# Four operand offsets in a decoder-layer kernel changed to two, and two of four weight combinations moved from VectorE to GpSimd

## The chip, the cores and the metric

The kernel runs on one core of a Trainium2 chip. The metric is the device time of one execution in microseconds (us): the median of three runs. One more execution was taken with the profiler on; all rows shown here come from it. Engines are named as in the profile: PE is TensorE's matmul, PEld its weight load, DVE is VectorE, ACT is ScalarE, POOL is GpSimd, SP is SyncE.

## The reference, cut to what matters

One decoder layer on 512 positions of width 2048, all in float32. Attention heads and a state-space mixer stand side by side, then a SwiGLU block of inner width 5632, then a last norm.

```
proj = rmsnorm(h) @ w_in                     # q, k, v, u: 4 x 1024
attn_out = dilated attention(q, k, v)        # 8 heads of 128
ssm_out  = y * sigmoid(y @ w_glu + b_glu)    # y: state-space scan over u, then GELU
h = h + concat(attn_out, ssm_out) @ w_out
hn = rmsnorm(h)
h = h + (silu(hn @ w_gate) * (hn @ w_up)) @ w_down
return rmsnorm(h)
```

## The kernel before

**Three matmuls for one product.** Everything is kept transposed: 128 features on the partitions, 512 positions along the row. A float32 operand is split into a high part (ScalarE copies it to the type that TensorE takes, `whi` for weights) and a rest (VectorE subtracts the high part from the raw value, `wlo`). A product is then three matmuls, lines 109 to 111 in `mm3`: high by high, high by rest, rest by high. `wsplit` makes the two parts of a 128x512 block of weights in buffers that are used in turn, five of each kind (`HB = 5`); the raw weights come by DMA from SP into four buffers of 1024 columns (`RAW = 4`).

**Slots for the moving operand.** The activations that stream through TensorE lie in slots of 1088 float32 a partition, of which 1024 are used: the high part and the rest. `laid(pool_, tag, name, bufs, o)` (line 167) gives a slot whose data begin `o` elements into it. There are three pools of such slots. In `ring` (tags A0, A1) lie the normed input `x`, then `attn`, `ssm`, `c1`, `c3`; in `ring2` (tag B) `ysp`, then `c2`; in `mp` (tags a, C) the SwiGLU outputs `m` and `c4`. Slots have one size, so two tiles of one pool and one `o` lie alike. The offsets are:

| operand | products | columns a matmul | pool | offset before |
|---|---|---|---|---|
| `x` | u, q, k, v | 512 | ring | 0 |
| `ysp` | glu | 512 | ring2 | 4 |
| `attn` | oa (first half of w_out) | 512 | ring | 8 |
| `ssm` | os (second half of w_out) | 256 | ring | 40 |
| `c1`, `c3` | gu products 1, 2, 5, 6 | 256 | ring | 48 |
| `c2` | gu products 3, 7 | 256 | ring2 | 48 |
| `c4` | gu product 4 | 256 | mp | 52 |
| `m` | dn (w_down), all groups but the last | 512 | mp | 0 |
| `m` | dl (w_down, last group) | 256 | mp | 48 |

**Gate and up with seven products.** For each of 44 tiles of 128 inner features, `gu(f)` computes gate and up together as a 2 by 2 block product in Winograd's form: seven products with combined weights and combined activations in place of eight. Each tile has two halves (`hh`), each with two DMAs of raw weights, `r1` (a11, a21) and `r2` (a22, a12). In a half, the weights of the products are, in the order in which they run on PE:

- A = a11 (product 1), C = a22 (product 4), B = a12 (product 2), as they come;
- D = a21 + a22 (product 5), written over a22;
- E = a11 - a21 (product 7), written over a21;
- F = D - a11 (product 6), written over a11;
- G = a12 - F (product 3), written over a12.

Each product is 12 matmuls of 256 columns: four blocks of weights, three matmuls each. The order of the lines in the program is that of `gu` (lines 738 to 749); the order of the instructions on each engine is set by the framework's scheduler, and each of DVE, ACT and POOL executes its own list in order. Lines 753 to 764 combine the seven results from four PSUM banks (seven adds of 256 columns and a multiply on VectorE) and split the output `m`.

**Order of the phases.** Eleven groups of four tiles. After the first tile of a group comes `down` for the group before: 16 output tiles of 12 matmuls with 512 columns. So on PE 192 matmuls of 512 columns alternate with runs of four tiles, 8 halves of 84 matmuls with 256 columns. Of the first five tiles the products A and B run ahead of the others (`gu_first`), while the loop at line 770 forms `c2`, `c3`, `c4` with VectorE and with GpSimd, which does four subtractions a step. The last `down` (`dl`) runs in two halves of 256 columns.

Of the kernel before, what the change touches and what calls it, by code (L numbers as in the profile page):

```python
# [15 lines left out]
ALU = mybir.AluOpType  # L16
# [19 lines left out]
def _emit(tc, a, y):  # L36
    nc = tc.nc
    act, dve, pool, pe = nc.scalar, nc.vector, nc.gpsimd, nc.tensor
    open_pools = {}

    def opened(name, **kw):
        cm = tc.tile_pool(name=name, **kw)
        open_pools[name] = cm
        return cm.__enter__()
# [4 lines left out]
    def tt(out, in0, in1, op, eng=None):  # L49
        (eng or dve).tensor_tensor(out=out, in0=in0, in1=in1, op=op)  # L50
# [23 lines left out]
    def acc(name):  # L74
        return psum.tile([128, 512], F32, tag="acc", name=name, bufs=5)
# [3 lines left out]
    def bank(name):  # L79

        turn[0] += 1
        return aux([128, 512], name) if turn[0] % 8 in (2, 5, 7) else acc(name)
# [6 lines left out]
    def split(hi, lo, raw):  # L89
        act.activation(hi, raw, AF.Copy)  # L90
        tt(lo, raw, hi.bitcast(F32), ALU.subtract)

    def wraw(src, name):
        raw = wpool.tile([128, 1024], F32, tag="raw", name="raw_" + name, bufs=RAW)
        nc.sync.dma_start(raw, src)
        return raw
# [16 lines left out]
    def ftile(ps, chunks, acts, name):  # L113
        n = len(chunks)
        for c, src in enumerate(chunks):
            ws = wchunk(src, f"{name}_{c}")
            for k in range(8):
                hi, lo = ws[k // 4]
                sl = slice(128 * (k % 4), 128 * (k % 4) + 128)
                mm3(ps, hi[:, sl], lo[:, sl], acts[8 * c + k], c == 0 and k == 0, c == n - 1 and k == 7)  # L120
# [43 lines left out]
    ring = opened("ring", bufs=1)  # L164
    SLOT = 1088

    def laid(pool_, tag, name, bufs, o):

        t = pool_.tile([128, SLOT], F32R, tag=tag, name=name, bufs=bufs)
        return t[:, o:o + 1024].rearrange("p (a b) -> p a b", a=2)  # L170

    def slot(tag, name, shift=0):
        return laid(ring, tag, name, 8, shift)
# [123 lines left out]
    for n in (1, 2, 4):  # L297
# [4 lines left out]
        t_ = pt[:, :, :n]  # L302
# [233 lines left out]
    ring2 = opened("ring2", bufs=1, side="right")  # L536
# [20 lines left out]
    ysp = []  # L557
    for b in range(8):
        yt = wpool.tile([128, 512], F32, tag="sq", name=f"yt{b}", bufs=4)
        nc.sync.dma_start(yt, sy[b].rearrange("p i c -> p (i c)"))  # L560
        t_ = laid(ring2, "B", f"ysp{b}", 8, 4)
        split(t_[:, 0, :], t_[:, 1, :], yt)
        ysp.append(t_)


    attn = []
    def scores(h):
        Pb = [slot("A1", f"P{h}_{i}").bitcast(F32) for i in range(2)]
        Tb = [slot("A1", f"PT{h}_{i}").bitcast(F32) for i in range(2)]
        for i in range(4):  # L570
            n = 128 * (i + 1)
            P = Pb[i // 2][:, i % 2, :]
            sps = aux([128, 512], f"sc{h}_{i}")
            pe.matmul(sps[:, :n], qs[h][:, 128 * i:128 * i + 128], ks[h][:, 0:n], start=True, stop=True)
            st = cpool.tile([128, 4], F32, tag="st", name=f"st{h}_{i}", bufs=4)
            dve.tensor_tensor_reduce(out=P[:, :n], in0=sps[:, :n], in1=mask[:, 512 - n:512], scale=1.0, scalar=-3e38,
                                     op0=ALU.add, op1=ALU.max, accum_out=st[:, 0:1])
            ts(st[:, 1:2], st[:, 0:1], -SCALE)
            act.activation(P[:, :n], P[:, :n], AF.Exp, bias=st[:, 1:2], scale=SCALE, accum_out=st[:, 2:3])
            dve.reciprocal(st[:, 3:4], st[:, 2:3])  # L580
            ts(P[:, :n], P[:, :n], st[:, 3:4])
        return Pb, Tb

    nxt = scores(0)
    for h in range(NH):
        Pb, Tb = nxt
        if h + 1 < NH:
            nxt = scores(h + 1)
        po = acc(f"po{h}")
        for step in "t0 t1 t2 p0 t3 p1 p2 p3".split():  # L590
            j = int(step[1])
            w = 512 - 128 * j
            PT = Tb[j // 2][:, j % 2, :]
            if step[0] == "t":
                tp = acc(f"tp{h}_{j}")
                for i in range(j, 4):
                    pe.transpose(tp[:, 128 * (i - j):128 * (i - j) + 128], Pb[i // 2][:, i % 2, 128 * j:128 * j + 128], ident)
                act.activation(PT[:, :w], tp[:, :w], AF.Copy)
            else:
                pe.matmul(po[:, 128 * j:512], vs[j][:, 128 * h:128 * h + 128], PT[:, :w], start=j == 0, stop=j == 3)  # L600
        o = slot("A0", f"attn{h}", 8)
        act.activation(o[:, 0, :], po, AF.Copy)
        tt(o[:, 1, :], po, o[:, 0, :].bitcast(F32), ALU.subtract)
        attn.append(o)


    ssm = []
    for f in range(8):
        ps = acc(f"glu{f}")
        ftile(ps, [a["w_glu"][f]], ysp, f"glu{f}")  # L610
        g_ = wpool.tile([128, 512], F32, tag="sq", name=f"gate{f}", bufs=4)
        act.activation(g_, ps, AF.Sigmoid, bias=bg[:, f:f + 1])
        yt = wpool.tile([128, 512], F32, tag="sq", name=f"yr{f}", bufs=4)
        nc.sync.dma_start(yt, sy[f].rearrange("p i c -> p (i c)"))
        z = wpool.tile([128, NC_, T], F32, tag="sq", name=f"gz{f}", bufs=4)
        tt(z.rearrange("p c i -> p i c"), yt.rearrange("p (i c) -> p i c", i=T), g_.rearrange("p (i c) -> p i c", i=T), ALU.mult)
        o = slot("A1", f"ssm{f}", 40)
        split(o[:, 0, :], o[:, 1, :], z.rearrange("p c i -> p (c i)"))
        ssm.append(o)
    closed("v")  # L620
# [6 lines left out]
    h = [hall[:, f, :] for f in range(KT)]  # L627
# [10 lines left out]

    def comb(tag, name, pool_=None, bufs=8):

        return laid(pool_ or ring, tag, name, bufs, 52 if tag == "C" else 48).rearrange("p a (h t) -> p a h t", h=2)

    early = {}

# [63 lines left out]
    def product(banks, i, hh, wh, wl):  # L708
        b_, j = REG[i]
        ps = banks[b_][:, E[j]]  # L710
        for k in range(4):
            sl = slice(128 * k, 128 * k + 128)
            mm3(ps, wh[:, sl], wl[:, sl], operand(i, 4 * hh + k), hh == 0 and k == 0 and i in (1, 5, 7, 4),
                hh == 1 and k == 3 and i in (2, 3, 6, 4))
# [16 lines left out]
    def gu(f, bank0=None):  # L731
        banks = [bank0 or bank(f"gu{f}_0")] + [bank(f"gu{f}_{i}") for i in range(1, 4)]
        for hh in range(2):
            r1 = wraw(a["w_gu"][f, hh, 0], f"r1_{f}_{hh}")
            r2 = wraw(a["w_gu"][f, hh, 1], f"r2_{f}_{hh}")
            a11, a21, a22, a12 = r1[:, W0], r1[:, W1], r2[:, W0], r2[:, W1]
            if bank0 is None:
                product(banks, 1, hh, *wsplit(a11, f"A{f}_{hh}"))
            product(banks, 4, hh, *wsplit(a22, f"C{f}_{hh}"))
            if bank0 is None:  # L740
                product(banks, 2, hh, *wsplit(a12, f"B{f}_{hh}"))
            tt(a22, a21, a22, ALU.add)
            product(banks, 5, hh, *wsplit(a22, f"D{f}_{hh}"))
            tt(a21, a11, a21, ALU.subtract)
            product(banks, 7, hh, *wsplit(a21, f"E{f}_{hh}"))
            tt(a11, a22, a11, ALU.subtract)
            product(banks, 6, hh, *wsplit(a11, f"F{f}_{hh}"))
            tt(a12, a12, a11, ALU.subtract)
            product(banks, 3, hh, *wsplit(a12, f"G{f}_{hh}"))
        P = {i: banks[b_][:, E[j]] for i, (b_, j) in REG.items()}  # L750
        g_ = wpool.tile([128, 512], F32, tag="sq", name=f"gt{f}", bufs=4)
        u_ = wpool.tile([128, 512], F32, tag="sq", name=f"up{f}", bufs=4)
        act.activation(g_[:, E[0]], P[1], AF.Copy)
        tt(u_[:, E[0]], g_[:, E[0]], P[6], ALU.add)
        tt(g_[:, E[0]], g_[:, E[0]], P[2], ALU.add)
        tt(g_[:, E[1]], u_[:, E[0]], P[5], ALU.add)
        tt(g_[:, E[1]], g_[:, E[1]], P[3], ALU.add)
        act.activation(g_, g_, AF.Silu)
        tt(u_[:, E[0]], u_[:, E[0]], P[7], ALU.add)
        tt(u_[:, E[1]], u_[:, E[0]], P[5], ALU.add)  # L760
        tt(u_[:, E[0]], u_[:, E[0]], P[4], ALU.add)
        tt(g_, g_, u_, ALU.mult)
        o = laid(mp, "a", f"m{f}", 4, 48 * (f >= 4 * (NPH - 1)))
        split(o[:, 0, :], o[:, 1, :], g_)
        return o
# [37 lines left out]
    for p in range(NPH):  # L803
        ms = []
        for q in range(4):
            f = 4 * p + q
# [114 lines left out]
```

## Time and profile before

| | |
|---|---|
| median of 3 runs | 2116.21 us (2115.62 to 2118.56) |
| the profiled execution's own time | 2112.28 us |
| its span, first to last instruction | 2110.5 us |
| mean granted TensorE clock | 0.986 |
| instructions | 35164, of which 13522 matmuls |

A row of the page's first part gives busy time, share of the span and number of instructions. A row of a timeline gives start, duration, engine, line, operation and tiles (out<-in). Matmuls overlap: one of 256 columns is shown 0.28 us long, while the next starts some 0.11 us behind its start, so the pace of PE is read from the distances of the starts, or from the number of matmuls in a stretch, and not from durations. The count in a stretch takes in those that reach over its ends: 1.7 (512 columns) or 2.4 (256 columns) too many, by duration over distance.

### The profile page before, as it was taken

How to read it: one execution, taken by the hardware profiler on the slowest of the kernel's cores; microseconds unless marked ns; L12 is line 12 of the kernel's file. 1: busy time of each engine (PE TensorE's matmuls, PEld its weight loads, DVE VectorE, ACT ScalarE, POOL GpSimd, SP SyncE). 2: the span in 40 equal slices, each digit the busy share in tenths (PEclk: the TensorE clock that was granted, in tenths of full speed). 3: DMA queues.
4: the chain of work that ended last, by engine and by line, in shares of the span. 5: the costliest groups of instructions: out<-in, count | busy, mean ns of one | idle time of the engine just before them, and what ended most of it. 6: DMA issues, size and time to landing. Idle time of an engine off the chain costs nothing.

```text
span 2110.5 us, 35164 instructions
## 1 busy us (share of the span) xinstructions
PE 2053.3 (97%) x13522; PEld 1858.4 (88%) x13522; DVE 1535.6 (73%) x2932; ACT 865.6 (41%) x1523; POOL 198.1 (9%) x172
## 2 busy tenths in 40 slices
PE   7899999999999979999999999999999999999996
PEld 5688888877889979899998989899998989999896
DVE  8835897555436989687786968687686868778686
ACT  5222222346325645344443535344352535444354
POOL 4533102300002360000000000000000000000002
PEclk9999999999999989999999999999999999999998
DMA  6443234623324614323232223323232332323232
GB/s 222 127 121 112 92 102 140 178 81 125 125 91 169 206 65 140 121 100 120 82 129 90 101 101 120 111 90 130 85 124 83 111 110 101 120 88 124 90 121 80
DMA packets 117193, 244.24 MB, mean 116 GB/s; under 512 B 39040, under 2 KB 57312, under 8 KB 117024
## 3 DMA queue, kind: packets, MB, share of 16 engines
q1 hardware_dynamic: 107808, 239.88, 33.8%
q10 hardware_dynamic: 9216, 2.10, 0.5%
q8 instruction: 106, 1.74, 0.3%
q14 instruction: 63, 0.52, 0.1%
HBM read 229.77 MB, written 9.03 MB: 113 GB/s over the span
## 4 chain that ended last, share of the span: by engine, by line
PE 87%; DVE 7%; issue 2%; DMA 1%; ACT 1%; SPq 0%; POOL 0%; DVEq 0%; ACTq 0%; POOLq 0%
PE gu L109 12%; PE gu L111 12%; PE gu L110 12%; PE dn L110 7%; PE dn L109 7%; PE dn L111 7%; PE lps L437 1%; PE q L111 1%; PE q L110 1%; PE oa L111 1%; PE oa L109 1%; PE oa L110 1%; PE q L109 1%; PE v L550 1%; PE v L552 1%
## 5 line engine op out<-in xcount | busy, mean ns | idle before, releaser
L110 PE MATMUL dn<-m,whi_dn 128*128 128x512 f32 x640 | 249.0, 389 | 0.0
L109 PE MATMUL dn<-m,whi_dn 128*128 128x512 f32 x640 | 248.8, 389 | 0.0
L111 PE MATMUL dn<-m,wlo_dn 128*128 128x512 f32 x640 | 248.8, 389 | 0.0
L50 DVE TENSOR_TENSOR h<-h,dn 128x512 f32<-128x512 f32 x160 | 109.9, 687 | 172.5 <-PE dn L111 171.3
L90 ACT ACTIVATE whi_dn<-raw_dn 128x512 fp32r<-128x512 f32 x160 | 100.9, 632 | 240.5 <-PE dn L110 208.2
L50 DVE TENSOR_TENSOR raw_r<-raw_r,raw_r 128x512 f32<-128x512 f32 x264 | 182.5, 691 | 2.2
L111 PEld LDWEIGHTS dn<-m,wlo_dn 128*128 128x128 f32 x640 | 120.2, 188 | 24.9
L109 PEld LDWEIGHTS dn<-m,whi_dn 128*128 128x128 f32 x640 | 120.2, 188 | 24.6
L110 PEld LDWEIGHTS dn<-m,whi_dn 128*128 128x128 f32 x640 | 120.2, 188 | 24.5
L50 POOL TENSOR_TENSOR h<-h,ssf 128x256 f32<-128x256 f32 x12 | 10.7, 920 | 1300.1 <-ACT ssf L160 1300.1
L50 DVE TENSOR_TENSOR wlo_dn<-raw_dn,whi_dn 128x512 fp32r<-128x512 f32 x160 | 109.8, 687 | 17.6 <-ACT whi_dn L90 16.5
L109 PE MATMUL gu<-c,whi_C 128*128 128x256 f32 x352 | 99.8, 284 | 1.9 <-ACT c L90 1.6
L111 PE MATMUL gu<-c,wlo_E 128*128 128x256 f32 x352 | 98.8, 281 | 2.8 <-DVE wlo_E L50 2.8
L109 PE MATMUL gu<-c,whi_D 128*128 128x256 f32 x352 | 98.3, 279 | 2.7 <-ACT whi_D L90 2.7
L109 PE MATMUL gu<-c,whi_E 128*128 128x256 f32 x352 | 98.5, 280 | 2.4 <-ACT whi_G L90 1.7
L111 PE MATMUL gu<-c,wlo_D 128*128 128x256 f32 x352 | 98.5, 280 | 2.0 <-DVE wlo_D L50 2.0
L111 PE MATMUL gu<-c,wlo_C 128*128 128x256 f32 x352 | 99.5, 283 | 0.5 <-DVE wlo_C L50 0.5
L110 PE MATMUL gu<-c,whi_C 128*128 128x256 f32 x352 | 99.6, 283 | 0.1
L110 PE MATMUL gu<-c,whi_E 128*128 128x256 f32 x352 | 98.3, 279 | 0.0
L110 PE MATMUL gu<-c,whi_D 128*128 128x256 f32 x352 | 98.0, 278 | 0.0
L109 PE MATMUL gu<-c,whi_F 128*128 128x256 f32 x352 | 97.7, 277 | 0.0
L109 PE MATMUL gu<-c,whi_G 128*128 128x256 f32 x352 | 97.5, 277 | 0.2 <-ACT whi_G L90 0.2
(323 smaller groups left out, 6673.1 us busy)
## 6 DMA issues: line engine op xcount, KB each, us to landing
raw_r<-w_gu SPq DMA_DIRECT2D x176, 512.0 KB, 3.6
raw_dn<-w_down SPq DMA_DIRECT2D x80, 512.0 KB, 4.1
raw_os<-w_out SPq DMA_DIRECT2D x32, 512.0 KB, 3.4
raw_q<-w_q SPq DMA_DIRECT2D x16, 512.0 KB, 3.5
raw_k<-w_k SPq DMA_DIRECT2D x16, 512.0 KB, 3.4
raw_v<-w_v SPq DMA_DIRECT2D x16, 512.0 KB, 3.7
raw_oa<-w_out SPq DMA_DIRECT2D x16, 512.0 KB, 3.5
raw_u<-w_u SPq DMA_DIRECT2D x15, 512.0 KB, 4.7
```

Of the source, the lines that this page charges most:

```text
L50: (eng or dve).tensor_tensor(out=out, in0=in0, in1=in1, op=op)
L90: act.activation(hi, raw, AF.Copy)
L109: pe.matmul(ps, wh, x[:, 0, :], start=first, stop=False)
L110: pe.matmul(ps, wh, x[:, 1, :], start=False, stop=False)
L111: pe.matmul(ps, wl, x[:, 0, :], start=False, stop=last)
L437: pe.matmul(lps[:, g, :], tm_[:, :, :, g].rearrange("p i q -> p (i q)"), U[:, 8 * b + g, :], start=True, stop=True)
L550: pe.matmul(pss[m], xs[kt][:, 0, ms], wh, start=kt == 0, stop=False)
L552: pe.matmul(pss[m], xs[kt][:, 1, ms], wh, start=False, stop=kt == 15)
```

## The change

Offsets: `ysp` 4 to 0, `attn` 8 to 0, `ssm` 40 to 48, `c4` 52 to 48. All 512-column operands then begin at 0 and all 256-column ones at 48. Sizes of tiles and pools stay as they are, so nothing else moves in memory. In `gu`, the subtractions that form E and G go from VectorE to GpSimd; D and F stay.

```
-        t_ = laid(ring2, "B", f"ysp{b}", 8, 4)
+        t_ = laid(ring2, "B", f"ysp{b}", 8, 0)
...
-        o = slot("A0", f"attn{h}", 8)
+        o = slot("A0", f"attn{h}")
...
-        o = slot("A1", f"ssm{f}", 40)
+        o = slot("A1", f"ssm{f}", 48)
...
-        return laid(pool_ or ring, tag, name, bufs, 52 if tag == "C" else 48).rearrange("p a (h t) -> p a h t", h=2)
+        return laid(pool_ or ring, tag, name, bufs, 48).rearrange("p a (h t) -> p a h t", h=2)
...
             product(banks, 5, hh, *wsplit(a22, f"D{f}_{hh}"))
-            tt(a21, a11, a21, ALU.subtract)
+            tt(a21, a11, a21, ALU.subtract, pool)
             product(banks, 7, hh, *wsplit(a21, f"E{f}_{hh}"))
             tt(a11, a22, a11, ALU.subtract)
             product(banks, 6, hh, *wsplit(a11, f"F{f}_{hh}"))
-            tt(a12, a12, a11, ALU.subtract)
+            tt(a12, a12, a11, ALU.subtract, pool)
             product(banks, 3, hh, *wsplit(a12, f"G{f}_{hh}"))
```

## Rows read from the trace of the kernel before

**Rows 1.** The page: busy time by engine, and the chain that ended last.

```profile
PE 2053.3 (97%) x13522; PEld 1858.4 (88%) x13522; DVE 1535.6 (73%) x2932; ACT 865.6 (41%) x1523; POOL 198.1 (9%) x172
...
PE 87%; DVE 7%; issue 2%; DMA 1%; ACT 1%; SPq 0%; POOL 0%; DVEq 0%; ACTq 0%; POOLq 0%
```

**Rows 2.** Stretches, all engines: stretch, its length, busy time (instructions), PE clock, DMA.

```profile
740.00:800.00 60.00, 48.14 (x333) 45.10 (x331) 53.54 (x80) 26.39 (x48) 33.64 (x32) 0.86 0.21 71
...
905.00:978.00 73.00, 73.00 (x641) 73.00 (x640) 62.68 (x111) 37.78 (x63) 0.00 (x0) 1.00 0.35 121
```

**Rows 3.** Stretches, PE alone: inside k, glu, oa, os (first half), dl.

```profile
280.00:330.00 50.00, 50.00 (x222) 1.00 0.29 100
515.00:545.00 30.00, 30.00 (x131) 1.00 0.38 132
560.00:630.00 70.00, 70.00 (x301) 1.00 0.30 102
645.00:685.00 40.00, 40.00 (x336) 1.00 0.54 184
2053.50:2069.50 16.00, 16.00 (x144) 1.00 0.01 2
```

**Rows 4.** Timeline of PE behind a down: first matmuls of products, two halves.

```profile
1503.30 0.28 PE L109 MATMUL gu<-c,whi_A 128*128 128x256 f32 x1
...
1504.71 0.28 PE L109 MATMUL gu<-c,whi_C 128*128 128x256 f32 x1
...
1506.13 0.28 PE L109 MATMUL gu<-c,whi_B 128*128 128x256 f32 x1
...
1507.51 0.28 PE L109 MATMUL gu<-c,whi_D 128*128 128x256 f32 x1
...
1512.95 0.28 PE L109 MATMUL gu<-c,whi_A 128*128 128x256 f32 x1
...
1514.31 0.28 PE L109 MATMUL gu<-c,whi_C 128*128 128x256 f32 x1
...
1522.56 0.28 PE L109 MATMUL gu<-c,whi_A 128*128 128x256 f32 x1
```

**Rows 5.** Timeline of PE in the first tiles: A and B alone, then F, G, C.

```profile
752.31 0.28 PE L109 MATMUL gu<-c,whi_A 128*128 128x256 f32 x1
...
757.96 0.28 PE L109 MATMUL gu<-c,whi_A 128*128 128x256 f32 x1
...
839.88 0.28 PE L109 MATMUL gu<-c,whi_F 128*128 128x256 f32 x1
...
841.29 0.28 PE L109 MATMUL gu<-c,whi_G 128*128 128x256 f32 x1
...
841.53 0.28 PE L109 MATMUL gu<-c,whi_C 128*128 128x256 f32 x1
...
842.24 0.28 PE L109 MATMUL gu<-c,whi_G 128*128 128x256 f32 x1
...
842.92 0.28 PE L111 MATMUL gu<-c,wlo_C 128*128 128x256 f32 x1
```

**Rows 6.** The page, costliest groups: combinations D, F, G on DVE.

```profile
L50 DVE TENSOR_TENSOR raw_r<-raw_r,raw_r 128x512 f32<-128x512 f32 x264 | 182.5, 691 | 2.2
```

**Rows 7.** DVE and POOL at one time (timelines), and POOL's 512-column groups.

```profile
399.67 1.78 DVE L50 TENSOR_TENSOR wlo_v<-raw_v,whi_v 128x512 fp32r<-128x512 f32 x1
...
399.28 1.63 POOL L50 TENSOR_TENSOR w<-w,wt 128x512 f32<-128x512 f32 x1
...
L50 POOL TENSOR_TENSOR w<-cc,pr 128x512 f32<-128x512 f32 x8 | 9.0, 1130 | 157.5 <-PE yps L517 131.5 <-DMA cc<-c_c 26.0
...
L50 POOL TENSOR_TENSOR wt<-cc,pi 128x512 f32<-128x512 f32 x8 | 15.1, 1886 | 13.6 <-issue 13.6
```

**Rows 8.** Timelines of DVE and PE: the last rest of G, and its first use.

```profile
1516.53 0.69 DVE L50 TENSOR_TENSOR wlo_G<-raw_r,whi_G 128x512 fp32r<-128x512 f32 x1 [0.73 <-ACT whi_G L90]
...
1521.43 0.28 PE L111 MATMUL gu<-c,wlo_G 128*128 128x256 f32 x1
```

## The prediction

> **What bounds the kernel now.** First the page: PE is busy 97% of the span and holds 87% of the chain that ended last; DVE is at 73%, GpSimd at 9% [rows 1]. Then the stretches, to see whether that average hides a stage with another bound. In the gate/up runs PE is busy for all of 73.00 us, DVE for 62.68 and GpSimd for none [rows 2]. The stretch from 740 to 800 us is the exception: there the second-half activations are formed, PE has 48.14 us of 60 at a granted clock of 0.86 (the mean of stretches at 2.4 and at 1.2 GHz), DVE 53.54 and GpSimd 33.64; DVE bounds it. Everywhere else a change is worth what it does to the pace of PE. Busy time cannot show that pace, so third the counts and starts of matmuls.
>
> The pace differs by operand. In 512 columns, k (offset 0) takes 50 us / (222 - 1.7) = 227.0 ns a matmul, glu (offset 4) 30 / 129.3 = 232.0, oa (offset 8) 70 / 299.3 = 233.9. In 256 columns, os (offset 40) takes 40 / (336 - 2.4) = 119.9 ns, dl (offset 48) 16 / 141.6 = 113.0 [rows 3].
>
> Offset 48 has two paces. In the timeline behind a down [rows 4], A takes 1.41 us for 12 matmuls (117.5 ns), C (offset 52) 1.42 (118.3), B 1.38 (115.0), then D, E, F, G 5.44 us for 48 (113.3); in the next half A takes 1.36 us (113.3). So the same operand, `c1` at 48, runs at 117.5 in one half and 113.3 in the next. Between the two stands C. The first tiles tell more [rows 5]. Where A and B run alone, with no C among them, 48 matmuls take 5.65 us, 117.7 ns, and the pace does not mend. F then takes 1.41 us for 12 (117.5), though it moves from `c2`'s pool to `c1`'s. At 841.53 two matmuls of C come in, and G behind them runs six matmuls in 0.68 us, 113.3 ns. I read this as two rhythms of PE at offset 48, short (113.3 ns) and long (117.7 ns), each of which keeps itself going. A down leaves the long rhythm behind; C, alone at another offset, costs 5 ns a matmul itself and throws PE into the short one.
>
> **The change part by part.** Offsets first.
>
> `attn` to 0: 384 matmuls of oa go from 233.9 to the 227.0 of k, whose `x` lies in the same pool at 0: -2.7 us. `ysp` to 0: 192 matmuls from 232.0 to 227.0: -1.0 us; that pool shows no 512-column operand at 0, so between 0 and -1.0.
>
> `ssm` to 48: os now comes behind 512-column matmuls, as A does behind a down, so I take the long rhythm: 384 matmuls of its first half from 119.9 to 117.7, -0.8 us, nothing for the second half. Were it short for both halves: 768 x 6.6 ns = -5.1 us.
>
> `c4` to 48 is the large term. It takes C's 118.3 ns away, and with it the step that ends the long rhythm. Behind each of ten downs come runs of tiles, 39 in all (5 to 43), so 78 halves of 84 matmuls. Now a half takes 9.65 us behind a down and 9.61 otherwise (1503.30 to 1512.95 to 1522.56 [rows 4]). All in the long rhythm: 84 x 117.7 = 9.89 us. That is 10 x 0.24 + 68 x 0.28 = +21.2 us. All in the short one: 84 x 113.3 = 9.52 us, 10 x -0.13 + 68 x -0.09 = -7.6 us. I take the long rhythm: the trace shows no stretch of it at 48 that mended without C, a PE stall or a matmul of another width, and in the gate/up runs PE has no stall [rows 2]. The ten halves of tiles 0 to 4, 60 matmuls each, lie between -0.8 and +1.8 us; stalls set the state there, and I take 0. The first half of dl, now at 113.0, inherits the long rhythm from the last run: 192 x 4.7 = +0.9 us.
>
> On this the Trainium skill (SBUF — State Buffer, Specifications) has a rule that would make the offsets equal: lines of 16 bytes. All of 4, 8, 40, 48 and 52 elements are whole numbers of such lines, so by it no operand is better placed than another, and the offset terms would sum to 0; the rows do not agree, 119.9 against 113.0 ns for 256 columns [rows 3].
>
> Now the 176 subtractions on GpSimd (88 halves, E and G). On DVE one takes 691 ns [rows 6]. GpSimd's 512-column groups run from 1130 to 1886 ns [rows 7]; I take 1.63, the row that stands beside a busy DVE. It also costs DVE: the split at 399.67 lasts 1.78 us where a DVE subtraction of this size lasts 0.69 [rows 7, 6], so 1.1 us is lost to GpSimd's one. Moving one then frees 0.7 and costs up to 1.1 us of DVE, +0.4. In a tile of 19.26 us DVE is busy 19.26 x 62.68 / 73 = 16.5 us [rows 2, 4]; four moved make it 18.1, under PE's 19.3 and under 19.8 in the long rhythm. GpSimd needs 4 x 1.63 = 6.5 us of the tile. The Trainium skill (SBUF — State Buffer, Who interferes with whom) speaks against the change more strongly: a VectorE instruction with two inputs in SBUF and a GpSimd one that reads SBUF exclude each other for the whole instruction. By that DVE would lose all of 1.63 us a subtraction, +0.94 net and 20.3 us a tile, which the lead below still covers; the row shows 1.1 lost.
>
> The chain grows too: D on DVE, E on GpSimd, F on DVE, G on GpSimd, then G's split. Twice 1.63 - 0.69, plus twice a DVE instruction that holds GpSimd off (0.69), is 3.3 us. What hides it: G's rest is ready at 1517.22 and first used at 1521.43, 4.2 us later [rows 8]. F waits on DVE for E, and behind it in DVE's list stand the splits of E, F and G and the adds that empty the PSUM banks; what is late next is the split of D or E, and PE only beyond 4 us. So 0 in the runs. From 740 to 800 us DVE has no such cover, and GpSimd already has 32 subtractions in its own list before E and G of the first tiles. Bounds: all 16 moved there shorten DVE, -11 us, or all lengthen it by 0.4 and PE waits for that, +6. I take +2, nearest to the contended row.
>
> **Sum.** 21.2 + 0.9 - 2.7 - 1.0 - 0.8 + 0 + 2 = +19.6 us. Against the profiled execution: 2112.3 + 19.6 = 2131.9. That execution is 3.9 us below the median of the runs, 2116.2, so for the median I say 2136.
>
> **The rivals.** *The short rhythm holds.* If `c4`'s other pool, or anything in the first half behind a down, ends the long rhythm without a change of offset, the runs take 113.3 ns. Then -7.6 - 0.8 - 2.7 - 1.0 - 5.1 + 2 = -15.2: 2101. For it: G to A passes from `c2` to `c1` in the short rhythm [rows 4], so all-48 does not break it. Against it: no A, B, E, F or G mended the long rhythm; only D, and the steps into and out of `c4` at 48, are untried. It decides once the long rhythm ends within the first quarter of a run (7.6 against 21.2). Chance 0.18.
>
> *Mixed, or offsets don't matter.* Stalls that GpSimd brings, or another order of the products, flip the rhythm about as often one way as the other, or the pace hangs on something other than the offset, as the rule of lines would have it. Half of each: (21.2 - 7.6) / 2 - 4.5 + 2 = +4: 2120; with no effect of offsets, +2: 2118. Rows 5 speak against both. Chance 0.14.
>
> *GpSimd becomes the bound.* If DVE, in order, waits out each GpSimd subtraction at the long end, a moved one costs 1.89 - 0.69 = 1.2 us of DVE. A tile in the long rhythm leaves 19.8 - 16.5 = 3.3 us, the lead gives 4.2 / 4 more, together 4.3 a tile or 1.08 an instruction: there it decides. At 1.2 a run of 16 loses 1.9 us, ten runs 19: 2116.2 + 19.6 + 19 = 2155. Two DVE instructions lie between E's subtraction and F's, which speaks against it. Chance 0.08.
>
> **How the numbers follow.** The forecast has 0.60, with a range of its own from 2128 (os in the short rhythm, the early tiles gaining) to 2143 (early tiles +1.8, 740 to 800 us at +6). No change that a measurement of this kernel can tell is 0.2%, 4.2 us. Slower: 0.60 + 0.08, and a little of the mixed case, 0.70; same 0.12; faster 0.18. To hold 8 in 10 the range reaches down to the short rhythm, 2100, and up to 2144, and leaves out the GpSimd case and the tails.
>
> **What the profile after would show.** Right: PE starts in a run 117.7 ns apart for all seven products, C with them, a period from down to down of some 123 us in place of 120; oa and glu at 227 ns; no waits of PE in the runs; DVE splits of 1.2 to 1.8 us beside GpSimd. Wrong: 113.3 ns from B or C on (the first rival), gaps of PE before E, F or G named after GpSimd or DVE (the GpSimd rival), or oa still at 234 ns. The prediction fails above all if something other than C's offset ends the long rhythm.

## The result, and the profile after

The kernel after takes 2140.36 us in the median of four runs (2137.94 to 2142.68), the kernel before 2115.91 in four runs of the same job (2113.49 to 2118.56): a ratio of 1.0115, interval 1.0096 to 1.0134. The forecast was 2136, slower, with a range of 2100 to 2144. The profiled execution took 2137.94 us with a span of 2136.2, 25.7 more than the span before.

The page of the kernel after, busy time and the chain, against [rows 1]:

```profile
PE 2069.0 (97%) x13522; PEld 1876.4 (88%) x13522; DVE 1544.6 (72%) x2756; ACT 863.7 (40%) x1523; POOL 465.6 (22%) x348
...
PE 58%; DVE 3%; ACT 1%; issue 0%; DMA 0%; POOL 0%; DVEq 0%; ACTq 0%; SPq 0%
```

The page alone would mislead. It shows the 176 subtractions on GpSimd (x172 to x348, 267 us more) and nothing of the 13522 matmuls, whose number is the same. That PE is busy 16 us longer with the same work is the hint. The chain's shares add up to 62%: here it is followed back through the last 1,300 us or so only, and its 58% is not to be set against the 87% of before.

The span is next cut where PE passes from one product to another (first matmul of oa, os, gu, the first and the last down). The six stages add up to the whole difference:

| stage | before, us | after, us | difference |
|---|---|---|---|
| start to oa (glu is in it) | 549.5 | 549.3 | -0.2 |
| oa | 89.6 | 87.0 | -2.6 |
| os | 95.5 | 94.7 | -0.8 |
| first gu matmul to first down ("first tiles") | 121.8 | 129.8 | +8.0 |
| first to last down (nine of the ten runs) | 1085.1 | 1105.2 | +20.1 |
| last down to the end | 169.0 | 170.2 | +1.2 |

glu lies in the first stage and takes 45.4 us before and 44.5 after, from its first matmul to that of oa. So it gains 0.9 us; but it begins 0.7 us later in the kernel after, and in the executions of this document it begins anywhere from 504.1 to 512.2 us.

Stretches of PE alone in the kernel after (stretch, length, busy time and count, clock, DMA), against the second, third and fourth of [rows 3]: glu and oa, then the first half of os.

```profile
515.00:545.00 30.00, 30.00 (x134) 1.00 0.38 132
...
560.00:630.00 70.00, 70.00 (x310) 1.00 0.29 102
645.00:685.00 40.00, 40.00 (x342) 1.00 0.55 188
```

With the correction of the counts as before: glu 30 / 132.3 = 226.8 ns a matmul, oa 70 / 308.3 = 227.1, os 40 / 339.6 = 117.8. The first two are now at the pace of k, and os has come to the long rhythm of 117.7, not to the short one.

Timeline of PE in the kernel after, behind a down: the first matmul of each product, against [rows 4].

```profile
1518.80 0.28 PE L109 MATMUL gu<-c,whi_A 128*128 128x256 f32 x1
...
1520.22 0.28 PE L109 MATMUL gu<-c,whi_C 128*128 128x256 f32 x1
...
1521.63 0.28 PE L109 MATMUL gu<-c,whi_B 128*128 128x256 f32 x1
...
1523.04 0.28 PE L109 MATMUL gu<-c,whi_D 128*128 128x256 f32 x1
...
1527.28 0.28 PE L109 MATMUL gu<-c,whi_G 128*128 128x256 f32 x1
...
1528.70 0.28 PE L109 MATMUL gu<-c,whi_A 128*128 128x256 f32 x1
...
1530.11 0.28 PE L109 MATMUL gu<-c,whi_C 128*128 128x256 f32 x1
...
1538.59 0.28 PE L109 MATMUL gu<-c,whi_A 128*128 128x256 f32 x1
```

Every product takes 1.41 or 1.42 us for 12 matmuls, 117.7 ns each, C among them, and a half 1528.70 - 1518.80 = 9.90 us. Nothing mends the long rhythm: it holds through all 39 tiles of the runs. Before, it was over in the first half [rows 4].

Stretches with all engines (PE, PEld, DVE, ACT, POOL), first tiles and a run of the kernel after, against [rows 2]:

```profile
731.00:862.40 131.40, 110.37 (x851) 104.69 (x850) 119.79 (x169) 58.81 (x105) 63.83 (x55) 0.94 0.30 103
910.00:983.00 73.00, 73.00 (x622) 73.00 (x622) 62.20 (x93) 36.82 (x62) 21.90 (x14) 1.00 0.33 115
```

The same first tiles in the kernel before:

```profile
734.60:858.00 123.40, 109.78 (x850) 105.56 (x849) 112.39 (x189) 58.76 (x105) 35.13 (x34) 0.93 0.32 110
```

In the run PE is busy for all of 73.00 us, with fewer matmuls in them than before (x622, not x641), and GpSimd's 21.90 us cost nobody anything that ends up on PE. In the first tiles PE does the same 850 matmuls in about the same busy time; its idle time grows from 123.40 - 109.78 = 13.6 to 131.40 - 110.37 = 21.0 us. DVE has 20 instructions fewer and is busy 7.4 us longer.

Groups of instructions of the kernel after: DVE's splits of D and E, then GpSimd's subtractions (E, then G). Busy time and mean ns stand behind the bar.

```profile
L50 DVE TENSOR_TENSOR wlo_E<-raw_r,whi_E 128x512 fp32r<-128x512 f32 x88 | 95.9, 1089 | 0.0
L50 DVE TENSOR_TENSOR wlo_D<-raw_r,whi_D 128x512 fp32r<-128x512 f32 x88 | 93.7, 1065 | 13.9 <-ACT whi_D L90 13.9
...
L50 DVE TENSOR_TENSOR wlo_G<-raw_r,whi_G 128x512 fp32r<-128x512 f32 x88 | 60.8, 691 | 16.1 <-ACT whi_G L90 12.0
```

```profile
L50 POOL TENSOR_TENSOR raw_r<-raw_r 128x512 f32<-128x512 f32 x88 | 140.5, 1597 | 896.9 <-DVE raw_r L50 882.2
...
L50 POOL TENSOR_TENSOR raw_r<-raw_r,raw_r 128x512 f32<-128x512 f32 x88 | 129.0, 1466 | 112.4 <-DVE raw_r L50 86.4
```

The splits that run beside a GpSimd subtraction grew to 1.07 and 1.09 us (0.69 before), that of F to 1.03; that of G, behind which GpSimd rests, kept its 0.691. GpSimd takes 1.47 to 1.60 us for one subtraction; the forecast took 1.63. The Trainium skill (SBUF — State Buffer, Who interferes with whom) states that one of the two holds the other off for the whole instruction. The trace agrees. Two pairs from the timelines of the kernel after:

```profile
1048.98 1.29 POOL L50 TENSOR_TENSOR raw_r<-raw_r,raw_r 128x512 f32<-128x512 f32 x1 [1.29 <-DVE raw_r L50]
1049.10 1.72 DVE L50 TENSOR_TENSOR wlo_E<-raw_r,whi_E 128x512 fp32r<-128x512 f32 x1
...
1056.66 1.62 POOL L50 TENSOR_TENSOR raw_r<-raw_r 128x512 f32<-128x512 f32 x1 [6.39 <-DVE raw_r L50]
1057.31 1.52 DVE L50 TENSOR_TENSOR wlo_D<-raw_r,whi_D 128x512 fp32r<-128x512 f32 x1 [0.18 <-ACT whi_D L90]
```

Each split ends 0.55 us behind the subtraction beside it (1050.82 and 1050.27, 1058.83 and 1058.28), though one begins 0.12 us into it and the other 0.65. So do 159 of the 170 splits of this trace that begin during a subtraction of E or G. A split thus loses what is left of GpSimd's instruction when it begins, not all of it. GpSimd waits in its turn: the second subtraction, which began while a split was running, took 1.62 us, the first 1.29. DVE's total gives the mean: 176 subtractions less (122 us by their means before) and still 9.0 us more busy time, so (122 + 9) / 176 = 0.74 us lost to each GpSimd subtraction.

Waits of PE in the kernel after, from 720 to 905 us (engine, line, what it waited for, us in total, times, longest):

```profile
PE gu L111 <- DVE wlo_D L50: 4.9, 4, 2.5
PE gu L111 <- DVE wlo_E L50: 4.8, 5, 1.9
PE gu L109 <- ACT whi_D L90: 3.2, 2, 1.9
PE gu L109 <- DVE up L50: 2.3, 2, 1.9
```

The same view of the kernel before has 2.8 us behind the rest of E and 2.0 behind that of D. What came late is thus the split of D or E, as the forecast said of a place without cover. From 860 to 2030 us, the runs, the view lists no wait of PE, before or after.

### The profile page after: what moved, and what is told of

Same layout as the page of the kernel before. It is cut to its first block, busy times and chain, and to the rows that moved or that the text cites. A ratio compares the mean times of both kernels' runs of the same rounds, so it can differ in the third digit from the quotient of the medians.

```text
span 2136.2 us, 35390 instructions
## 1 busy us (share of the span) xinstructions
PE 2069.0 (97%) x13522; PEld 1876.4 (88%) x13522; DVE 1544.6 (72%) x2756; ACT 863.7 (40%) x1523; POOL 465.6 (22%) x348
## 4 chain that ended last, share of the span: by engine, by line
PE 58%; DVE 3%; ACT 1%; issue 0%; DMA 0%; POOL 0%; DVEq 0%; ACTq 0%; SPq 0%
PE gu L109 12%; PE gu L111 12%; PE gu L110 12%; PE dn L109 7%; PE dn L111 7%; PE dn L110 7%; DVE h L50 1%; DVE wlo_E L50 0%; DVE wlo_D L50 0%; PE dl L109 0%; PE dl L111 0%; PE dl L110 0%; DVE gt L50 0%; DMA raw_dl<-w_down 0%; DVE up L50 0%
## 5 line engine op out<-in xcount | busy, mean ns | idle before, releaser
L50 POOL TENSOR_TENSOR raw_r<-raw_r 128x512 f32<-128x512 f32 x88 | 140.5, 1597 | 896.9 <-DVE raw_r L50 882.2
L50 POOL TENSOR_TENSOR raw_r<-raw_r,raw_r 128x512 f32<-128x512 f32 x88 | 129.0, 1466 | 112.4 <-DVE raw_r L50 86.4
L50 DVE TENSOR_TENSOR raw_r<-raw_r,raw_r 128x512 f32<-128x512 f32 x176 | 121.4, 690 | 1.8
L50 DVE TENSOR_TENSOR wlo_F<-raw_r,whi_F 128x512 fp32r<-128x512 f32 x88 | 90.3, 1027 | 19.6 <-ACT whi_F L90 19.6
L50 DVE TENSOR_TENSOR wlo_D<-raw_r,whi_D 128x512 fp32r<-128x512 f32 x88 | 93.7, 1065 | 13.9 <-ACT whi_D L90 13.9
L111 PE MATMUL gu<-c,wlo_F 128*128 128x256 f32 x352 | 99.5, 283 | 0.9 <-DVE wlo_F L50 0.9
L110 PE MATMUL gu<-c,whi_C 128*128 128x256 f32 x352 | 99.1, 281 | 1.0 <-DVE c L50 0.8
```

The lines of the kernel that those rows point to most:

```text
L110: pe.matmul(ps, wh, x[:, 1, :], start=False, stop=False)
L111: pe.matmul(ps, wl, x[:, 0, :], start=False, stop=last)
```

## The experiments

All medians are of several rounds on the same chip as runs of the kernel before; the ratio is against those. The stages are of the profiled execution, in us, "rest" from the last down to the end.

| kernel | median, us | before | ratio, interval | oa | first tiles | first to last down | down to down | rest |
|---|---|---|---|---|---|---|---|---|
| before | | | | 89.6 | 121.8 | 1085.1 | 120.44 | 169.0 |
| after | 2140.36 | 2115.91 | 1.0115 [1.0096, 1.0134] | 87.0 | 129.8 | 1105.2 | 122.67 | 170.2 |
| c4 alone | 2140.63 | 2116.97 | 1.0110 [1.0092, 1.0128] | 89.6 | 121.8 | 1105.2 | 122.67 | 170.4 |
| GpSimd alone | 2124.95 | 2116.97 | 1.0046 [1.0029, 1.0064] | 89.6 | 130.0 | 1085.1 | 120.44 | 168.1 |
| after, c4 back at 52 | 2119.54 | 2116.97 | 1.0012 [1.0001, 1.0024] | 87.0 | 129.7 | 1085.1 | 120.44 | 169.0 |
| four offsets alone | 2131.54 | 2116.97 | 1.0074 [1.0059, 1.0089] | 87.0 | 122.2 | 1105.2 | 122.67 | 169.7 |
| three offsets alone | 2111.89 | 2116.01 | 0.9978 [0.9968, 0.9988] | 87.0 | 122.6 | 1085.1 | 120.44 | 170.6 |
| GpSimd from tile 5 on | 2131.77 | 2116.01 | 1.0072 [1.0055, 1.0088] | 87.0 | 122.0 | 1105.2 | 122.67 | 169.4 |
| D, E, F, G on GpSimd | 2147.86 | 2116.01 | 1.0146 [1.0131, 1.0161] | 87.0 | 134.3 | 1105.2 | 122.67 | 173.7 |
| first c4 tile at 52 | 2106.68 | 2116.01 | 0.9955 [0.9941, 0.9969] | 87.0 | 122.0 | 1081.3 | 120.01 | 169.1 |
| first c4 tile at 0 | 2107.03 | 2114.29 | 0.9967 [0.9954, 0.9979] | 87.0 | 122.4 | 1080.4 | 119.92 | 167.6 |
| first c4 tile at 56 | 2133.82 | 2114.29 | 1.0096 [1.0081, 1.0112] | 87.0 | 121.8 | 1105.4 | 122.69 | 169.8 |
| first c4 tile at 40 | 2121.21 | 2116.56 | 1.0018 [1.0006, 1.0029] | 87.0 | 122.0 | 1093.2 | 121.34 | 169.9 |
| c1 to c4 at 0 | 2148.17 | 2114.29 | 1.0161 [1.0147, 1.0174] | 87.0 | 123.9 | 1118.8 | 124.18 | 171.5 |

The medians add up only to some 5 us: `c4` alone (+23.7) and three offsets alone (-4.1) would make +19.5, and the four offsets measure +14.6. The time before glu alone differs by up to 8 us between executions, so the argument goes by the stages behind it.

The theory at the start: `c4`'s offset sets the runs, GpSimd costs only where DVE is the bound, and the other three offsets give a few us. The rivals: GpSimd, with its waits on DVE, makes the rhythm long or delays the runs; or the offsets do nothing.

### The parts one by one

**`c4` at 48, nothing else**, against the kernel before:

```
-        return laid(pool_ or ring, tag, name, bufs, 52 if tag == "C" else 48)...
+        return laid(pool_ or ring, tag, name, bufs, 48)...
```

> The kernel before with one edit: c4 at offset 48. Theory of the two rhythms: with no operand at another offset a run stays at 117.7 ns a matmul behind every down; the period from down to down goes from 120.4 to about 122.7 us, the time up by 20 to 22 us, to about 2137. Rival, GpSimd beside PE holds the long rhythm: no GpSimd work in the runs here, so products A to G take 113.3 ns, the period falls to about 119.8, the time to about 2109.

This one number brings the whole +20.1 us of the runs (1105.2, the period 122.67) and leaves oa and the first tiles as they were. A stretch of PE inside the first run:

```profile
910.00:980.00 70.00, 70.00 (x597) 1.00 0.30 108
```

70 / (597 - 2.4) = 117.7 ns. GpSimd does no combination here, so it does not make the rhythm long.

**E and G on GpSimd, nothing else**, against the kernel before:

```
-            tt(a21, a11, a21, ALU.subtract)
+            tt(a21, a11, a21, ALU.subtract, pool)
...
-            tt(a12, a12, a11, ALU.subtract)
+            tt(a12, a12, a11, ALU.subtract, pool)
```

> The kernel before with the subtractions for E and G on GpSimd, all offsets as before. Theory of the two rhythms: the runs keep their period of 120.4 us, PE has no wait in them, and the whole cost, 6 to 9 us, lies between the first gate/up matmul and the first down (123.4 us before, about 131 here); time about 2123. Rival, GpSimd holds the long rhythm: period near 122.6, time about 2144.

The first tiles grow by 8.2 us to 130.0, and the runs stay at 1085.1 to the tenth of a us. The first tiles of this kernel, all engines:

```profile
737.40:867.40 130.00, 111.49 (x838) 106.40 (x837) 117.60 (x166) 57.88 (x103) 63.85 (x54) 0.91 0.29 100
```

As in the kernel after, DVE has fewer instructions and more busy time than before (117.60 us, not 112.39), and PE is idle for 18.5 us, not 13.6.

**The kernel after with `c4` back at 52:**

```
-        return laid(pool_ or ring, tag, name, bufs, 48)...
+        return laid(pool_ or ring, tag, name, bufs, 52 if tag == "C" else 48)...
```

> The changed kernel with c4 back at 52. Theory of the two rhythms: period back at 120.4 us, C and the first matmuls behind it at 115 to 118 ns, the rest at 113.3; time 21 us under the changed kernel, about 2119. Rival, GpSimd holds the long rhythm: period stays above 122, time above 2138.

The runs are back at 1085.1, with the 176 subtractions still on GpSimd. From both sides, then: with `c4` at 52 the runs take 1085.1, with `c4` at 48 they take 1105.2, whatever GpSimd does.

**The four offsets without GpSimd**: the two edits of `gu` undone in the kernel after.

```
-            tt(a21, a11, a21, ALU.subtract, pool)
+            tt(a21, a11, a21, ALU.subtract)
...
-            tt(a12, a12, a11, ALU.subtract, pool)
+            tt(a12, a12, a11, ALU.subtract)
```

> The changed kernel with E and G back on VectorE. Theory of the two rhythms: runs unchanged against the changed kernel (period 122.7 us), the stretch from the first gate/up matmul to the first down back to about 124 us; time about 8 us under the changed kernel, 2132, and 16 above the kernel before. Rival, GpSimd holds the long rhythm: all of A to G at 113.3 ns, time about 2103.

The first tiles fall back to 122.2 us, the runs stay at 1105.2, oa at 87.0. Each engine executes the same list in the same order as in the kernel before, so order has no part in the 20.1 us of the runs.

**Three offsets alone** (`ysp` 0, `attn` 0, `ssm` 48; `c4` stays at 52, and all combinations stay on VectorE):

```
-        t_ = laid(ring2, "B", f"ysp{b}", 8, 4)
+        t_ = laid(ring2, "B", f"ysp{b}", 8, 0)
...
-        o = slot("A0", f"attn{h}", 8)
+        o = slot("A0", f"attn{h}")
...
-        o = slot("A1", f"ssm{f}", 40)
+        o = slot("A1", f"ssm{f}", 48)
```

> The kernel before with ysp at 0, attn at 0 and ssm at 48; c4 stays at 52, the combinations on VectorE. Theory of the two rhythms: glu, oa and os give back 0.9, 2.5 and 0.9 us, the period stays at 120.4; time 4.3 us under the kernel before, 2112. Rival, the mixture of offsets as such keeps a run quick and evening them out harms anywhere: os or oa no quicker than before, time 2116 or above.

4.1 us less than before, the good part of the change: glu gives its 0.9 us here too, and oa its 2.6. os as a whole gives nothing in this execution (95.5 us, as before), though its first half takes 45.2 us as in the kernel after (46.1 before). The second half takes 50.2 us, not 49.4: PE waits 1.8 us for DVE before the broadcast matmul of the norm (`bc`), 1.0 in the kernel after.

### GpSimd: where it costs

**GpSimd only from tile 5 on**, that is in the runs and not in the first tiles, in the kernel after:

```
-            tt(a21, a11, a21, ALU.subtract, pool)
+            tt(a21, a11, a21, ALU.subtract, pool if f >= NEARLY else dve)
...
-            tt(a12, a12, a11, ALU.subtract, pool)
+            tt(a12, a12, a11, ALU.subtract, pool if f >= NEARLY else dve)
```

> The changed kernel with GpSimd forming E and G only from tile 5 on. Theory: GpSimd's cost lies in the first five tiles alone, where VectorE bounds; the stretch from the first gate/up matmul to the first down goes from 130 back to about 122 us, the period stays at 122.7, time 2132, as with no GpSimd subtraction at all. Rival, GpSimd costs as much wherever it stands: 156 of 176 subtractions remain, the time stays within 2 us of the changed kernel, 2139.

The first tiles are back at 122.0 us, and the median is that of the four offsets without GpSimd (2131.77 and 2131.54, at 15.8 and 14.6 above their own runs of before). So 20 of the 176 moved subtractions bring everything that GpSimd costs; the other 156 neither cost nor give anything.

How the 20 cost it is less certain. DVE's idle time in the first tiles is nearly the same before and after (123.40 - 112.39 = 11.0 and 131.40 - 119.79 = 11.6 us), so the stage grew by DVE's busy time. But with the 20 on GpSimd the scheduler also gives the first tiles another order: 148 of PE's matmuls there stand at another place in its list, and the lists of DVE and ScalarE change too, while the kernel of this run keeps the order of before up to the first down. And the chain that ended last in the kernel after has two GpSimd subtractions of 1.63 us on it (at 807 and 841 us), beside the lengthened splits of D and E. No run parts the three.

**All four combinations on GpSimd**, D and F too, in the kernel after:

```
-            tt(a22, a21, a22, ALU.add)
+            tt(a22, a21, a22, ALU.add, pool)
...
-            tt(a11, a22, a11, ALU.subtract)
+            tt(a11, a22, a11, ALU.subtract, pool)
```

> The changed kernel with all four combinations, D and F too, on GpSimd. Theory: what hides GpSimd in the runs is the lead of the weights, some 4 us, and VectorE's spare time. With four a tile costs VectorE 8 x 0.37 = 3 us net on 16.5, 19.5 of 19.8, and the chain of four grows by 4 x 0.9 us to the end of the lead: single waits of PE before D to G in the runs, period 122.7 to 124, the first tiles 8 us longer still; time 2148 to 2165. Rival, the lead is wide enough for any order of engines: period 122.67 as before, no wait of PE in the runs, time about 2148.

This one went against me as to the runs, where I looked for single waits of PE; there are none from 870 to 2060 us, and the period is 122.67 to the hundredth. The first tiles, and a stretch of a run, in this kernel:

```profile
735.10:869.40 134.30, 114.39 (x838) 106.57 (x837) 115.31 (x146) 58.61 (x104) 92.71 (x75) 0.91 0.28 97
...
917.00:990.00 73.00, 73.00 (x622) 73.00 (x622) 63.67 (x80) 36.62 (x62) 43.10 (x28) 1.00 0.29 104
```

GpSimd is busy for 43.10 us of 73, DVE for 63.67, only 1.5 more than with two combinations moved (62.20), and PE for all of it. In the first tiles, 4.5 us longer than in the kernel after, DVE's busy time falls from 119.79 to 115.31; there it waits for the high part of D (6.1 us in total, 0.8 in the kernel after), and ScalarE, which makes that part, waits for GpSimd before it (19.0 us in total). By these waits the chain through GpSimd, and no longer DVE's busy time, delays the first tiles with four moved; no run tests it.

### What ends the long rhythm

**Only the first tile of `c4` at 52.** `c4` is four tiles of two blocks each, so the first one streams through 6 of the 84 matmuls of a tile's first half, and through none of the second (where an expectation below counts 3, 6 is right). The other offsets as in the change, no combination on GpSimd:

```
-        return laid(pool_ or ring, tag, name, bufs, 48)...
+        return laid(pool_ or ring, tag, name, bufs, 52 if name == "c4_0" else 48)...
```

> As the three offsets, but of the four c4 tiles only the first (two of eight blocks of K) lies at 52, the others at 48. Theory of the two rhythms: one visit to another offset is enough to end the long rhythm, so six matmuls a tile pay in place of 24; the period falls from 120.4 to about 120.0 us, the time to about 2107 to 2108, under both kernels. Rival, it takes the whole of C at 52 (the rhythm comes back with c4 at 48): a period between 121 and 122.7 us, time 2118 to 2134.

Timeline of PE in this kernel behind a down, first matmuls of products:

```profile
1498.07 0.28 PE L109 MATMUL gu<-c,whi_A 128*128 128x256 f32 x1
...
1499.48 0.28 PE L109 MATMUL gu<-c,whi_C 128*128 128x256 f32 x1
...
1500.91 0.28 PE L109 MATMUL gu<-c,whi_B 128*128 128x256 f32 x1
...
1502.27 0.28 PE L109 MATMUL gu<-c,whi_D 128*128 128x256 f32 x1
...
1507.71 0.28 PE L109 MATMUL gu<-c,whi_A 128*128 128x256 f32 x1
...
1509.07 0.28 PE L109 MATMUL gu<-c,whi_C 128*128 128x256 f32 x1
...
1510.43 0.28 PE L109 MATMUL gu<-c,whi_B 128*128 128x256 f32 x1
```

A at 117.5 ns, C with its six matmuls at 52 at 119, and from B on 1.36 us a product, 113.3 ns; in the second half C, all at 48, takes 1.36 us too. A run now pays for the long rhythm in one product, and for a visit in four. The median, 2106.68, lies under both kernels.

**The same tile at 0, at 56 and at 40** asks whether any step will do.

```
+        return laid(pool_ or ring, tag, name, bufs, 0 if name == "c4_0" else 48)...
```

(56, 40 in the other two.)

> The four offsets of the change, no combination on GpSimd, and of c4 only its first tile (3 of the 84 matmuls of a half, in the first half of each gate/up tile alone) at offset 0 where all other 256-column operands are at 48. Theory (the step to another offset and back ends the long rhythm, whatever that offset is): as with that tile at 52, the long rhythm only from a down to the first C, then 113.3 ns; a period from down to down of 120.0 us, a median of 2105 to 2109. Rival (it is something of offset 52, not the step): the long rhythm through all runs, a period of 122.7 us, 2131, as with all of c4 at 48.

> The same with the first tile of c4 at offset 56. Theory: again 120.0 us from down to down, 2105 to 2109. Rival (only some offsets end it): 122.7 us and 2131; if 0 ends it and 56 does not, or the other way round, the step alone is not the cause.

> As the runs with the first tile of c4 (6 matmuls of a gate/up tile) at 52, 0 or 56, now at 40. Theory (the long rhythm ends at an offset that has another pace of its own: 0 with 119.9 ns and 52 with 118 to 119 end it, 56 keeps 117.7 and does not): 40 had 119.9 ns in os before, so it ends it; 120.0 us from down to down, a median of 2105 to 2109. Rival (a step of 8 elements, as from 48 to 56, is too small to end it): 122.7 us, 2131 to 2134.

At 0 it ends as at 52: 119.92 us from down to down, and 2107.03. At 56 it does not, and the simple form of the theory falls. Timeline of PE with the tile at 56, behind a down:

```profile
1513.35 0.28 PE L109 MATMUL gu<-c,whi_A 128*128 128x256 f32 x1
...
1514.77 0.28 PE L109 MATMUL gu<-c,whi_C 128*128 128x256 f32 x1
...
1516.18 0.28 PE L109 MATMUL gu<-c,whi_B 128*128 128x256 f32 x1
...
1517.60 0.28 PE L109 MATMUL gu<-c,whi_D 128*128 128x256 f32 x1
```

C takes 1.41 us like any other product, and B behind it too. I then thought that an offset ends the rhythm if it has another pace of its own. At 40, whose pace was 119.9 ns [rows 3], neither theory held. Timeline with the tile at 40: first the first tile of a run, then its third.

```profile
1505.58 0.28 PE L109 MATMUL gu<-c,whi_A 128*128 128x256 f32 x1
...
1506.99 0.28 PE L109 MATMUL gu<-c,whi_C 128*128 128x256 f32 x1
...
1508.42 0.28 PE L109 MATMUL gu<-c,whi_B 128*128 128x256 f32 x1
...
1509.83 0.28 PE L109 MATMUL gu<-c,whi_D 128*128 128x256 f32 x1
...
1546.58 0.28 PE L109 MATMUL gu<-c,whi_C 128*128 128x256 f32 x1
...
1547.99 0.28 PE L109 MATMUL gu<-c,whi_B 128*128 128x256 f32 x1
...
1549.35 0.28 PE L109 MATMUL gu<-c,whi_D 128*128 128x256 f32 x1
```

In the first tile B behind C keeps its 1.41 us; in the third B takes 1.36. It is so in every one of the ten runs: four halves at 117.8 ns a matmul, the fifth mends behind its C, and then 113.3 to the end of the run, but for the C of the fourth tile. The same visit to the same offset thus fails twice and succeeds the third time, always at the same place.

**`c1` to `c4` all at 0:**

```
+        return laid(pool_ or ring, tag, name, bufs, 0)...
```

> The four offsets of the change, no combination on GpSimd, and c1, c2, c3 and c4 all at offset 0 (ssm and the last group of m stay at 48). Theory (the rhythms belong to PE and its history, not to offset 48; without a step between offsets none ends): all seven products at one pace near 117.7 ns in all runs, 122.7 us from down to down, 2131. Rival (the long rhythm is a property of offset 48, and at 0 the pace is short whatever comes before): 84 matmuls of 113.3 ns a half, 119.6 us from down to down, about 2103. A third: offset 0 is slower for 256 columns, as 40 is; at 119.9 ns a matmul 124.2 us, about 2145.

The third case that the expectation names: a stretch of PE inside the first run of this kernel.

```profile
905.00:975.00 70.00, 70.00 (x586) 1.00 0.32 106
```

70 / (586 - 2.4) = 119.9 ns, with all starts 120 ns apart. For 256 columns 0 is a worse place than 48 in either of its rhythms, while it is the best of the three offsets seen for 512.

## Why the prediction was right, and where it was off

The mechanism and the sign held, and the terms can be set against the stages.

- **`c4`, +21.2 in the runs and +0.9 in dl.** The long rhythm held for all seven products of all 39 tiles. From down to down the forecast's 0.24 + 7 x 0.28 = 2.2 us were 122.67 - 120.44 = 2.23. Nine runs lie between the first and the last down: 19.6 of the forecast's 21.2 (the last run, of three tiles, has 0.24 + 5 x 0.28 = 1.6), 20.1 measured. That last run and dl make 1.6 + 0.9 = 2.5 of the forecast, 1.2 measured: in the first part of dl the pace was 118 ns only until a stall some 45 matmuls into it, and then 113 for the most part. `c4` alone brought the whole 20.1, and taking it back took the whole away: this is shown. The forecast needed only that nothing else in a run ends the long rhythm. That any step to another offset ends it, as I thought later, is not so (56, 40).
- **`attn`, -2.7, and `ysp`, -1.0.** oa gave 2.6 and glu 0.9 in every run that has the edits. At the start of oa only 0.2 of the 0.9 are left in the kernel after, because glu began 0.7 us later there; in the three executions without these edits it begins between 504.1 and 506.4 us.
- **`ssm`, -0.8.** Measured -0.8, with the first half at 117.8 ns as forecast: 45.2 us in every run with the edit, 46.1 without. The second half varies with its waits, from 49.1 to 50.5 us with the edit, so os as a whole gave anything from 1.2 less to 0.2 more.
- **GpSimd in the runs, 0.** Right: 156 of the moved subtractions change nothing, and even four moved leave no wait on PE. The cost to DVE that I used there was too high: a tile should have had 18.1 us of DVE; 62.20 / 73 of its 19.8 us are 16.9. The splits beside GpSimd came to 1.03 to 1.09 us in the mean, under the 1.2 to 1.8 that I looked for. I also priced the rule of the Trainium skill (SBUF — State Buffer, Who interferes with whom) as if DVE lost all of GpSimd's 1.63 us; the pairs above show that it loses what is left when a split begins.
- **The first tiles, +2 with bounds of -11 and +6: the term that was mis-sized.** It was +8.0 in the kernel after, 8.2 with GpSimd alone, and gone when GpSimd starts with tile 5. Two errors. I counted 16 subtractions; five tiles of two halves have 20. And I took +2 as nearest to the contended row, though that row, +0.4 us of DVE for one moved, gives the whole of the bound where DVE is the bound: 20 x 0.4 = 8.0. DVE's busy time there rose by 7.4 us, 0.37 for each one moved: freed 0.69, lost 1.06, and the row of the forecast said 1.1. The sizes agree, but that DVE's loss is the whole cause is argued: the order of the first tiles changed with it.

The sum was +19.6, the spans differ by 25.7: of the 6.1 us between them 6.0 are the first tiles, and the rest nearly cancels: 0.8 less gained up to oa (0.7 of it before glu begins), 0.1 of oa and 0.5 more in nine runs, against 1.3 less in the last run and dl. Of the rivals, the short rhythm was excluded by the starts in the runs, mixed rhythms by one pace in all 39 tiles, and GpSimd as the bound by a full PE in the runs.

## What to carry to other kernels

Price a moved instruction by the stage in which each copy of it runs: the same subtraction cost nothing 156 times and, with the other order that came along, 0.4 us 20 times, and the stage where its engine is the bound is where to count first and exactly. When a change makes operands uniform, ask whether an irregularity was doing something, and try more than one other value, for 56 did nothing here: at 52 six matmuls a tile are worth some 24 us (2131.54 is 14.6 above its own runs of before, 2106.68 is 9.3 below them). And read PE's pace from the distances of starts, product by product, in stretches where it never waits; busy time showed 97% in both kernels.

## What the runs showed of the hardware

- With the operand at 48 elements, 256-column matmuls run 113.3 or 117.7 ns apart, and each rhythm keeps itself going, the short one for the 150 matmuls and more between two visits, the long one for a whole run of 672, with the clock at 1.00 and no wait. A down of 512-column matmuls leaves the long one behind, every time.
- Six matmuls at 52 or at 0 end the long one at the first visit in all ten runs, six at 56 never, and six at 40 only at the third visit, at the same place in all ten runs. That fits two stable positions in a cycle between which a visit shifts PE by an amount that depends on the offset; this is argued, not shown, and what inside PE or its reads makes the cycle stays open.
- By pace, offsets rank differently for the two widths: 512 columns at 0, 4 and 8 elements take 227.0, 232.0 and 233.9 ns, 256 columns at 0 take 119.9, more than either rhythm at 48. The Trainium skill (SBUF — State Buffer, Specifications) has lines of 16 bytes; all these offsets are whole lines, so the rule does not tell them apart, and the measurements do.
- A DVE split that begins during a GpSimd subtraction, both with two inputs in SBUF, ends 0.55 us behind its end (159 of 170 in the kernel after). DVE's mean loss to a GpSimd subtraction of 1.5 us was 1.06 us in the first tiles, where DVE is busy for 119.79 of 131.40 us, and (131 - 21) / 156 = 0.70 in the rest of the kernel.
